# Expert products in source order: gate and up by turns, and expert 0's gather one row block ahead

## The chip, the cores and the metric

The kernel runs on one core of one Trainium2 chip. The metric is device time in microseconds (us), taken over runs of the same program.

## The reference, cut to what matters

One layer over 512 latent tokens of width 1024 with 256 context tokens: a mixer (projection, recurrence, attention, output projection), then routed experts. The change touches only the experts. Each of 16 experts takes the 64 tokens that score highest for it, and its three weight matrices (1024 x 2816, 1024 x 2816, 2816 x 1024, float32) are read once.

```
def expert_choice_ffn(h, w_router, w_gate, w_up, w_down):
    aff = jax.nn.softmax((h @ w_router).astype(jnp.float32), axis=-1)
    g, idx = lax.top_k(jnp.swapaxes(aff, 1, 2), cap)          # cap = 64
    xe = jax.vmap(lambda hb, ib: hb[ib])(h, idx)
    def expert(args):
        xk, wg, wu, wd = args
        return (jax.nn.silu(xk @ wg) * (xk @ wu)) @ wd
    ...
```

## The kernel before, in words

Up to about 448 us the mixer and the router run; their instructions are recorded in a `Flow` object and issued in the order of its list schedule (helper line 254 in the profile). Then come the experts.

The weights of an expert come in 24 loads, issued by SP (SyncE): for each of eight row blocks k (128 rows of the gate and of the up matrix) one load of gate and one of up, then eight loads of the down matrix, three blocks of 128 rows in each but the last. Each load fills one of 14 slots of SBUF, taken in turn (`slot`); a load waits until the products that read its slot's former content are done. One expert is 34.6 MB (3 x 1024 x 2816 x 4 bytes).

`gather` builds the input of two experts at once: for each of the eight k, four products with a one-hot matrix (`oh`), made by eight VectorE instructions, into a PSUM bank (`y` and `tr` by turns), and a ScalarE instruction that writes `xe[:, k]`. `gates` takes the gate values and the token numbers by small products and VectorE copies.

`up_part` multiplies: for each k, for each of six chunks of columns (five of 512, one of 256), for hh = 0 (gate) and 1 (up), one product into the bank `gu` of that chunk. Gate writes PSUM partitions 0 to 63 of the bank, up writes 64 to 127, so the two use different halves of TensorE's columns:

```
pe.matmul(b[hh * 64:(hh + 1) * 64, :n], xe[:, k, es], wgu[k][hh][:, f:f + n],
          start=(k == 0), stop=(k == KT - 1), skip_group_check=True)
```

A float32 product stands in the trace as two passes, so a row block's 12 products are 24 passes.

`down_part` takes each chunk through SiLU (ScalarE), the multiply by up (VectorE), transposes (TensorE, bank `tr`) and a copy to `hT` (ScalarE); then 22 times two products with the down weights go into the bank `y`, each pair to the two halves; then the scaling (VectorE) and an indirect DMA from GpSimd that adds the 64 rows to the output.

What sets the order: expert 0's gather and `up_part` are recorded in the `Flow`, with a `bias` that falls by 100 for each k, and go out in its list schedule. From expert 0's `down_part` on, instructions are given straight to the engines outside of a manual schedule, and the framework's scheduler may put those of one engine in another order than they are written.

Of the kernel before, what the change touches and what calls it, by code (L numbers as in the profile page):

```python
# [42 lines left out]
class Flow:  # L43
    """Records the instructions of a phase, orders them by a list schedule of their data
    dependences and issues them in that order; Tile still draws every wait."""
# [78 lines left out]
    def copy(self, o, i):  # L124
        """A copy on whichever of ScalarE and VectorE is free first."""
        self.add("act", "activation", (o, i, AF.Copy), {}, [("vec", "tensor_copy", (o, i), {})])

    def affine(self, o, i, scale, bias):
        """scale * i + bias, a column each, on ScalarE or VectorE."""
        self.add("act", "activation", (o, i, AF.Identity), {"scale": scale, "bias": bias},  # L130
                 [("vec", "tensor_scalar", (o, i, scale, bias), {"op0": OP.mult, "op1": OP.add})])

    def tt(self, o, a, b, op):
        """A tensor_tensor in SBUF on whichever of VectorE and GpSimd is free first."""
        self.add("vec", "tensor_tensor", (o, a, b), {"op": op}, [("gp", "tensor_tensor", (o, a, b), {"op": op})])
# [88 lines left out]
    def flush(self):  # L224
        """Issues what was recorded in the order of a list schedule, by the longest path to the end."""
        ops, self.ops = self.ops, []
        for name, op in self.waits:
            for rec in self.acc[name]:
                self.link(rec[0], op)
        self.waits = []  # L230
        deps = {o["i"]: o["n"] for o in ops}
        topo = [o for o in ops if not o["n"]]
        for o in topo:
            for s, _ in o["to"].values():
                deps[s["i"]] -= 1
                if not deps[s["i"]]:
                    topo.append(s)
        assert len(topo) == len(ops)
        for op in reversed(topo):
            c = min(v[3] for v in op["alt"].values())  # L240
            if op["e"] == "sp":
                c += 2.5 + op["bytes"] / 360e3
            op["c"] = c
            op["lvl"] = op["boost"] + max([c, 0.0] + [s["lvl"] + (0.0 if issue else c)
                                                      for s, issue in op["to"].values()])
        for op in ops:
            op["lvl"] += op["bias"]
        order, self.free, self.dma_free, self.act_set = self.schedule(ops)
        for o, e, st, end in order:
            o["e"], o["st"], o["end"] = e, st, end  # L250
            o["m"], o["a"], o["k"], o["cost"] = o["alt"][e]
        with self.tc.manual_schedule():
            for o, e, st, end in order:
                getattr(self.eng[e], o["m"])(*o["a"], **o["k"])  # L254
# [58 lines left out]
def hybrid_block_kernel(ctx: ExitStack, tc: tile.TileContext, x, cx, w_ada, b_ada, w_in, w_out, w_router, w_gate,  # L313
# [23 lines left out]
    def carve(slot):  # L337
        """Small tiles out of a slot that the experts' weights take over."""
        flat, end = slot.rearrange("p a d -> p (a d)"), [0]

        def part(shape):
            n = int(np.prod(shape[1:]))
            v = flat[:shape[0], end[0]:end[0] + n]
            end[0] += n
            assert end[0] <= 3 * D
            dims = "abc"[:len(shape) - 1]
            return v if len(shape) == 2 else v.rearrange(f"p ({' '.join(dims)}) -> p {' '.join(dims)}",
                                                         **{d: k for d, k in zip(dims, shape[1:])})
        return part
# [18 lines left out]
    def load_ex(e, k, i):  # L368
        """Rows of an expert's gate (i = 0) or up weights."""
# [24 lines left out]
    def split(h, l, src):  # L394
        """src as the sum of two float32r parts."""
        copy(h, src)
        tt(l, src, h.bitcast(F32), OP.subtract)

# [61 lines left out]
    # start clears the accumulation flags of its whole bank, so only the first product in a bank sets it  # L460
    def chan_chunk(w, with_ctx, kouter=False):
        """Two channel tiles of 512 latent tokens, a bank each, and their 256 context tokens in a third one."""
# [119 lines left out]
    def tok_chunk(w, with_ctx):  # L582
        """256 columns of two token tiles to a bank."""
# [34 lines left out]
    # tables of the rotary embedding with the norms' gains, [token, tile, dim]  # L618
# [31 lines left out]
    # softplus(-lambda) as max(-lambda, 0) + 2 atanh(t / (2 + t)), t = exp(-|lambda|)  # L650
# [92 lines left out]
    def qk_post(v, t, tb, kind, dst):  # L743
        """Norm and rotation of token tiles t, t + 1 in bank v, 256 columns each; keys as float32r parts, transposed."""
# [194 lines left out]
    # w_out as two float32r parts in place of the input projection's operands  # L939
# [19 lines left out]
    def mix_parts(t, parts):  # L959
        """The mixer's output for token tile t as float32r parts; parts: (tiles of lru and att, H, L)."""  # L960
# [63 lines left out]
    # logits = rstd * (x1 (A2 w)) + B2 w  # L1024
# [37 lines left out]
    # the 64 largest, sorted, of the first two tiles, then of these and the third tile, and of the fourth tile  # L1062
# [31 lines left out]
    # of two sorted rows the 64th largest is the largest of min(i-th of one, (64 - i)-th of the other)  # L1094
# [18 lines left out]
    # tokens above the least one taken, and of those equal to it the first ones, as many as are left to take  # L1113
# [15 lines left out]
    def count(o, m, stop):  # L1129
        """How many tokens up to each one have m, for each expert."""  # L1130
# [13 lines left out]
    # over the norms, by which the gathering products are scaled  # L1144
# [21 lines left out]
    def gather(pair):  # L1166
        """The tokens of two experts, normed and modulated, one column each."""
        xe = E.tile([128, KT, 128], F32, name="xe", bufs=1)
# [5 lines left out]
        for k in range(KT):  # L1174
            flow.bias = 2050.0 - 100 * k
            pg = etr([128, 128]) if k % 2 else pe_ps.tile([128, 128], F32, name="y", tag="y", bufs=1)
            for t in range(4):
                pe.matmul(pg, X1[t][:, k * 128:(k + 1) * 128], oh[:, t].rearrange("p i s -> p (i s)"),  # L1178
                          start=(t == 0), stop=(t == 3))
            act.activation(xe[:, k], pg, AF.Identity, bias=B2[:, k:k + 1], scale=A2[:, k:k + 1])  # L1180
        flow.bias = 0.0
        return xe, oh

    def gates(pair, oh):
        """The gate values of the taken tokens of two experts (twice, below each other) and the tokens' numbers."""
# [16 lines left out]
    def up_part(xe, i, wgu):  # L1202
        gu = [pe_ps.tile([128, 512], F32, name="gu", tag="gu", bufs=6) for _ in FC]
        es = slice(i * CAP, (i + 1) * CAP)
        for k in range(KT):
            flow.bias = 2000.0 - 100 * k
            for (f, n), b in zip(FC, gu):
                for hh in range(2):
                    pe.matmul(b[hh * 64:(hh + 1) * 64, :n], xe[:, k, es], wgu[k][hh][:, f:f + n],  # L1209
                              start=(k == 0), stop=(k == KT - 1), skip_group_check=True)  # L1210
        flow.bias = 0.0
        return gu

    def down_part(gu, wd, g_t, ix):
        hT = E.tile([128, NF, CAP], F32, name="hT", tag="hT", bufs=1)
        y = pe_ps.tile([128, 512], F32, name="y", tag="y", bufs=1)
        for (f, n), b in zip(FC, gu):
# [7 lines left out]
        for ff in range(NF):  # L1225
            for hh in range(2):
                pe.matmul(y[hh * 64:(hh + 1) * 64, :], hT[:, ff], wd[ff][:, hh * 512:(hh + 1) * 512],  # L1227
                          start=(ff == 0), stop=(ff == NF - 1), skip_group_check=True)
# [7 lines left out]

    wgu, wd = load_gu(0), load_dn(0)
    xe, oh = gather(0)
    gu = up_part(xe, 0, wgu)
    gx = gates(0, oh)  # L1240
    flow.flush()
    act, vec, gp, pe, sp = nc.scalar, nc.vector, nc.gpsimd, nc.tensor, nc.sync
    down_part(gu, wd, *gx[0])
    for e in range(1, NE):
        wgu, wd = load_gu(e), load_dn(e)
        cur = gx[e % 2]
        gu = up_part(xe, e % 2, wgu)
        if e % 2 == 1 and e + 1 < NE:
            xe, oh = gather((e + 1) // 2)
            gx = gates((e + 1) // 2, oh)  # L1250
        down_part(gu, wd, *cur)
# [9 lines left out]
def _layout(inputs):  # L1261
    """The small parameters side by side, as the kernel loads them."""
# [4 lines left out]
    # [channel tile, block of the tile, in, direction, gate, out]  # L1267
# [37 lines left out]
```

## Time and profile before

| | |
|---|---|
| median of 3 runs | 1779.17 us (1779.17, 1779.17, 1780.07) |
| profiled execution, first to last instruction | 1780.5 us |
| PE (TensorE products) busy | 1644.3 us, 92% |
| DVE (VectorE), ACT (ScalarE), POOL (GpSimd) busy | 387.6, 323.0, 132.5 us |
| bytes moved by DMA | 607.33 MB |
| granted TensorE clock, mean | 0.969 |

The profiled execution's span is its own time; it is 0.07% above the median of the runs shown, and sums are made against it. A busy PE is not a PE at its peak, since the ends of products are modelled. SP's busy time is not counted; its queue is seen in the timeline of its issues. A granted clock of 1.00 is 2.4 GHz, 0.50 is 1.2 GHz.

### The profile page before, as it was taken

Reading aid. Unit: us, or ns where it says so; the run is one execution under the profiler, and the core shown is the slowest. Engines: PE = TensorE matmul, PEld = TensorE weight load, DVE = VectorE, ACT = ScalarE, POOL = GpSimd, SP = SyncE. Lnnn points to the kernel's source line nnn. Section 1 sums busy time; section 2 is a strip of 40 time slices with the busy share of each in tenths; the row PEclk is TensorE's granted clock in tenths of the full one; section 3 lists DMA queues with packets and bytes.
Section 4 is the critical chain, followed back from the end, with each engine's and each line's share of the span. In section 5 each row is a group of like instructions: output and inputs, shape, how many; then the busy total and the mean of one; then the engine's idle time right before and its main releaser. Section 6 shows DMA issues by size and latency. Waiting matters only on the chain.

```text
span 1780.5 us, 19112 instructions
## 1 busy us (share of the span) xinstructions
PE 1644.3 (92%) x8030; PEld 798.7 (45%) x8030; DVE 387.6 (22%) x788; ACT 323.0 (18%) x607; POOL 132.5 (7%) x143
## 2 busy tenths in 40 slices
PE   7999988883899999999999999999999999999997
PEld 4567787672433433344343334333433433343332
DVE  5667786724110100010010001010100010000001
ACT  5256755520010101020010102010100101020101
POOL 2141153300000000000000000000000000000000
PEclk9999999896899999999999999999999999999999
DMA  9563112255689999999999999999999999999997
GB/s 346 173 225 107 36 36 83 78 190 207 260 324 363 419 401 423 417 426 416 420 420 423 421 422 420 422 414 426 420 420 420 423 420 420 423 420 422 421 422 293
DMA packets 116900, 607.33 MB, mean 341 GB/s; under 512 B 12393, under 2 KB 31046, under 8 KB 84046
## 3 DMA queue, kind: packets, MB, share of 16 engines
q1 hardware_dynamic: 115534, 601.91, 83.1%
q0 software_dynamic: 1280, 4.20, 1.2%
q8 instruction: 63, 1.03, 0.2%
q14 instruction: 23, 0.19, 0.0%
HBM read 599.78 MB, written 6.29 MB: 340 GB/s over the span
## 4 chain that ended last, share of the span: by engine, by line
PE 49%; DMA 35%; issue 6%; DVE 6%; ACT 2%; POOL 1%; SPq 0%; POOLq 0%; ACTq 0%; DVEq 0%
PE gu L1209 18%; DMA r<-in_w_up_dram 16%; DMA ring<-in_w_up_dram 9%; PE y L1227 9%; PE ac L254 7%; DMA r<-in_w_down_dram 5%; PE gu L254 3%; DMA ring<-in_w_down_dram 3%; PE pv L254 3%; PE p L254 2%; PE tr L254 1%; PE tr L1223 1%; PE y L1178 1%; DVE ring L254 1%; PE tr L1178 1%
## 5 line engine op out<-in xcount | busy, mean ns | idle before, releaser
L1209 PE MATMUL gu<-r,xe 128*64 128x512 f32 (+1 forms) x1656 | 479.6, 560 | 5.9 <-DMA r<-in_w_up_dram 4.9
L1209 PE MATMUL gu<-ring,xe 128*64 128x512 f32 (+1 forms) x1224 | 365.8, 560 | 3.2 <-DMA ring<-in_w_up_dram 3.2
L1209 PEld LDWEIGHTS gu<-r,xe 128*64 128x64 f32 x1656 | 173.9, 137 | 275.9 <-issue 252.9
L1220 DVE TENSOR_TENSOR sg<-sg,gu 64x512 f32<-64x512 f32 x96 | 61.7, 647 | 785.3 <-ACT sg L1219 785.1
L1219 ACT ACTIVATE sg<-gu 64x512 f32<-64x512 f32 x96 | 52.7, 553 | 984.6 <-PE gu L1209 977.7
L1209 PEld LDWEIGHTS gu<-ring,xe 128*64 128x64 f32 x1224 | 131.4, 136 | 202.1 <-issue 187.1
L1227 PE MATMUL y<-r,hT 128*64 128x512 f32 x812 | 210.3, 617 | 0.6 <-DMA r<-in_w_down_dram 0.6
L1227 PE MATMUL y<-ring,hT 128*64 128x512 f32 x596 | 151.7, 606 | 1.2 <-DMA ring<-in_w_down_dram 1.2
L1234 POOL DMA_INDIRECT out_dram<-ys,ix x16 | 22.8, 1426 | 1313.2 <-DVE ys L1233 1313.2
L254 PE MATMUL ac<-w,ring 128*128 128x256 f32 x768 | 108.2, 290 | 1.1 <-DVE w L254 0.7
L1227 PEld LDWEIGHTS y<-r,hT 128*64 128x64 f32 x812 | 58.8, 139 | 99.3 <-issue 90.3
L254 PEld LDWEIGHTS ac<-w,ring 128*128 128x128 f32 x768 | 97.4, 190 | 12.8 <-issue 11.2
L1233 DVE SCALAR_TENSOR_TENSOR ys<-y,gate,brow 64x512 f32<-64x512 f32 x32 | 24.0, 749 | 294.9 <-PE y L1227 294.6
L1227 PEld LDWEIGHTS y<-ring,hT 128*64 128x64 f32 x596 | 43.7, 138 | 75.5 <-issue 69.0
L254 PE MATMUL ac<-ring,w 128*128 128x512 f32 (+1 forms) x240 | 68.4, 395 | 0.2 <-ACT V L254 0.2
L1223 PEld LDWEIGHTS tr<-ident,sg 64*128 64x128 f32 x352 | 30.5, 145 | 77.7 <-ACT hT L1224 40.6
L1223 PE MATMUL tr<-ident,sg 64*128 64x64 f32 x352 | 43.7, 244 | 13.8 <-ACT hT L1224 8.3
L1224 ACT ACTIVATE hT<-tr 128x256 f32<-128x256 f32 x96 | 35.1, 366 | 103.5 <-PE tr L1223 97.8
L254 PEld LDWEIGHTS ac<-ring,w 128*128 128x128 f32 x240 | 40.9, 194 | 8.6 <-issue 3.4
L1178 PE MATMUL y<-oh,raw 128*128 128x128 f32 x224 | 31.0, 281 | 14.6 <-DVE ys L1233 10.4
L254 ACT ACT_TABLE_LOAD x32 | 41.1, 1283 | 8.1 <-DVE lru L254 6.8
L254 PE MATMUL p<-kS,qs 128*128 128x256 f32 (+1 forms) x128 | 33.7, 378 | 5.4 <-ACT e L254 5.4
(250 smaller groups left out, 1263.7 us busy)
## 6 DMA issues: line engine op xcount, KB each, us to landing
r<-in_w_gate_dram SPq DMA_DIRECT2D x73, 1408.0 KB, 26.0
r<-in_w_up_dram SPq DMA_DIRECT2D x73, 1408.0 KB, 26.6
r<-in_w_down_dram SPq DMA_DIRECT2D x64, 1536.0 KB, 21.1
ring<-in_w_gate_dram SPq DMA_DIRECT2D x55, 1408.0 KB, 25.9
ring<-in_w_up_dram SPq DMA_DIRECT2D x55, 1408.0 KB, 26.5
ring<-in_w_down_dram SPq DMA_DIRECT2D x47, 1536.0 KB, 20.9
raw<-in_w_ada_dram SPq DMA_DIRECT2D x32, 512.0 KB, 4.7
raw<-in_w_in_dram SPq DMA_DIRECT2D x20, 512.0 KB, 4.7
```

The costliest lines, as they stand in the source:

```text
L254: getattr(self.eng[e], o["m"])(*o["a"], **o["k"])
L1178: pe.matmul(pg, X1[t][:, k * 128:(k + 1) * 128], oh[:, t].rearrange("p i s -> p (i s)"), start=(t == 0), stop=(t == 3))
L1209: pe.matmul(b[hh * 64:(hh + 1) * 64, :n], xe[:, k, es], wgu[k][hh][:, f:f + n], start=(k == 0), stop=(k == KT - 1), skip_group_check=True)
L1219: act.activation(sg[64:128, :n], b[:64, :n], AF.Silu)
L1220: vec.tensor_tensor(sg[64:128, :n], sg[64:128, :n], b[64:128, :n], op=OP.mult)
L1223: pe.transpose(pt[:, j], sg[64:128, j * 128:(j + 1) * 128], ident[64:128, 64:128])
L1224: act.activation(hT[:, f // 128:f // 128 + n // 128], pt[:, :n // 128], AF.Copy)
L1227: pe.matmul(y[hh * 64:(hh + 1) * 64, :], hT[:, ff], wd[ff][:, hh * 512:(hh + 1) * 512], start=(ff == 0), stop=(ff == NF - 1), skip_group_c ...
L1233: vec.scalar_tensor_tensor(ys[:, cs_], y[pp, :], g_t[pp, :], m5row[pp, :], op0=OP.mult, op1=OP.mult)
L1234: gp.indirect_dma_start(out=out, out_offset=bass.IndirectOffsetOnAxis(ap=ix[:, :1], axis=0), in_=ys, in_offset=None, compute_op=OP.add)
```

## The change

Three things. Expert 0's gather and products are no longer recorded in the `Flow`: they are written out as gather block 0, then for each k gather block k + 1 and the products of row block k. All expert work is put inside a manual schedule, so that each engine gets its instructions as written: gate and up by turns in every chunk, the gather for the next two experts as one piece after an odd expert's row blocks. And `down_part` writes the down products of chunk c - 1 behind chunk c's transposes and copy. The mixer, the router, the loads' order on SP and the arithmetic are the same.

```
-    def up_part(xe, i, wgu):
-        gu = [pe_ps.tile([128, 512], F32, name="gu", tag="gu", bufs=6) for _ in FC]
+    def up_rows(gu, xe, i, wgu, k):
         es = slice(i * CAP, (i + 1) * CAP)
-        for k in range(KT):
-            flow.bias = 2000.0 - 100 * k
-            for (f, n), b in zip(FC, gu):
-                for hh in range(2):
-                    pe.matmul(b[hh * 64:(hh + 1) * 64, :n], xe[:, k, es], wgu[k][hh][:, f:f + n],
-                              start=(k == 0), stop=(k == KT - 1), skip_group_check=True)
+        for (f, n), b in zip(FC, gu):
+            for hh in range(2):
+                pe.matmul(b[hh * 64:(hh + 1) * 64, :n], xe[:, k, es], wgu[k][hh][:, f:f + n],
+                          start=(k == 0), stop=(k == KT - 1), skip_group_check=True)
...
             act.activation(hT[:, f // 128:f // 128 + n // 128], pt[:, :n // 128], AF.Copy)
-        for ff in range(NF):
-            for hh in range(2):
-                pe.matmul(y[hh * 64:(hh + 1) * 64, :], hT[:, ff], wd[ff][:, hh * 512:(hh + 1) * 512],
-                          start=(ff == 0), stop=(ff == NF - 1), skip_group_check=True)
+            if c:
+                products(*FC[c - 1])
+        products(*FC[-1])
...
     wgu, wd = load_gu(0), load_dn(0)
-    xe, oh = gather(0)
-    gu = up_part(xe, 0, wgu)
-    gx = gates(0, oh)
+    oh = one_hot(0)
     flow.flush()
     act, vec, gp, pe, sp = nc.scalar, nc.vector, nc.gpsimd, nc.tensor, nc.sync
-    down_part(gu, wd, *gx[0])
-    for e in range(1, NE):
-        wgu, wd = load_gu(e), load_dn(e)
-        cur = gx[e % 2]
-        gu = up_part(xe, e % 2, wgu)
-        if e % 2 == 1 and e + 1 < NE:
-            xe, oh = gather((e + 1) // 2)
-            gx = gates((e + 1) // 2, oh)
-        down_part(gu, wd, *cur)
+    with tc.manual_schedule():
+        for e in range(NE):
+            if e == 0:
+                xe, gu = new_xe(), banks()
+                gather(xe, oh, 0)
+                for k in range(KT):
+                    if k + 1 < KT:
+                        gather(xe, oh, k + 1)
+                    up_rows(gu, xe, 0, wgu, k)
+                gx = gates(0, oh)
+                cur = gx[0]
+            else:
+                wgu, wd = load_gu(e), load_dn(e)
+                cur = gx[e % 2]
+                gu = banks()
+                for k in range(KT):
+                    up_rows(gu, xe, e % 2, wgu, k)
+                if e % 2 == 1 and e + 1 < NE:
+                    oh = one_hot((e + 1) // 2)
+                    xe = new_xe()
+                    for k in range(KT):
+                        gather(xe, oh, k)
+                    gx = gates((e + 1) // 2, oh)
+            down_part(gu, wd, *cur)
```

What this does to the order on PE, at expert 0's row block 3 (`ring1_3763` is its gate block, `ring1_3764` its up block, `gu_...` the six banks). Before:

```order
L254 MATMUL gu_3791<-ring1_3763,xe_3781 64x512
L254 MATMUL gu_3792<-ring1_3763,xe_3781 64x512
L254 MATMUL gu_3793<-ring1_3763,xe_3781 64x512
L254 MATMUL gu_3794<-ring1_3763,xe_3781 64x512
L254 MATMUL gu_3795<-ring1_3763,xe_3781 64x512
L254 MATMUL gu_3796<-ring1_3763,xe_3781 64x256
L254 MATMUL gu_3791<-ring1_3764,xe_3781 64x512
L254 MATMUL gu_3792<-ring1_3764,xe_3781 64x512
L254 MATMUL gu_3793<-ring1_3764,xe_3781 64x512
L254 MATMUL gu_3794<-ring1_3764,xe_3781 64x512
L254 MATMUL gu_3795<-ring1_3764,xe_3781 64x512
L254 MATMUL gu_3796<-ring1_3764,xe_3781 64x256
```

The same row block with the change:

```order
L1209 MATMUL gu_3843<-ring1_3763,xe_3842 64x512
L1209 MATMUL gu_3843<-ring1_3764,xe_3842 64x512
L1209 MATMUL gu_3844<-ring1_3763,xe_3842 64x512
L1209 MATMUL gu_3844<-ring1_3764,xe_3842 64x512
L1209 MATMUL gu_3845<-ring1_3763,xe_3842 64x512
L1209 MATMUL gu_3845<-ring1_3764,xe_3842 64x512
L1209 MATMUL gu_3846<-ring1_3763,xe_3842 64x512
L1209 MATMUL gu_3846<-ring1_3764,xe_3842 64x512
L1209 MATMUL gu_3847<-ring1_3763,xe_3842 64x512
L1209 MATMUL gu_3847<-ring1_3764,xe_3842 64x512
L1209 MATMUL gu_3848<-ring1_3763,xe_3842 64x256
L1209 MATMUL gu_3848<-ring1_3764,xe_3842 64x256
```

Six gate products and then six up products became pairs of the two. Before, 3 of the 128 row blocks stood fully by turns (one in expert 0, its block 5), 56 fully one after the other, the rest in between; now all 128 stand by turns.

The second place is ScalarE at the end of expert 0's row blocks (`sg` is the SiLU's result, `hT` the transposed chunk, `tr` the bank of the transposes). Before:

```order
L1219 ACTIVATE sg_4019<-gu_3791 64x512
L1219 ACTIVATE sg_4028<-gu_3792 64x512
L1224 ACTIVATE hT_4017<-tr_4022 128x256
L1219 ACTIVATE sg_4037<-gu_3793 64x512
L1224 ACTIVATE hT_4017<-tr_4031 128x256
```

With the change:

```order
L1224 ACTIVATE sg_4021<-gu_3843 64x512
L1229 ACTIVATE hT_4019<-tr_4024 128x256
L1224 ACTIVATE sg_4030<-gu_3844 64x512
L1229 ACTIVATE hT_4019<-tr_4033 128x256
L1224 ACTIVATE sg_4047<-gu_3845 64x512
```

The second chunk's SiLU stood ahead of the first chunk's copy to `hT`, and now stands behind it. So it is in every expert.

## Rows read from the trace of the kernel before

**Rows 1.** The page, section 2: mean busy share of the DMA engines in 40 slices:
```profile
DMA  9563112255689999999999999999999999999997
```

**Rows 2.** Stretches: length, busy us of PE, PEld, DVE, ACT, POOL, clock, DMA share, GB/s:
```profile
460.00:540.00 80.00, 76.30 (x314) 30.94 (x312) 6.10 (x18) 9.99 (x20) 0.00 (x0) 0.96 0.77 294
480.00:500.00 20.00, 20.00 (x69) 7.97 (x67) 0.00 (x0) 0.91 (x2) 0.00 (x0) 1.00 0.99 376
540.00:640.00 100.00, 97.22 (x469) 40.49 (x466) 7.78 (x20) 9.06 (x20) 1.77 (x1) 0.97 1.00 409
640.00:1740.00 1100.00, 1058.70 (x4663) 420.29 (x4662) 83.54 (x170) 92.51 (x204) 19.65 (x14) 0.99 1.01 421
```

**Rows 3.** Timeline of SP's queue, 440 to 545: start, us, the loads it issues:
```profile
464.29 0.33 SPq L254 DMA_DIRECT2D ring<-in_w_gate_dram  x1
...
472.87 9.49 SPq L254 DMA_DIRECT2D r<-in_w_down_dram  x4
...
506.72 0.34 SPq L371 DMA_DIRECT2D r<-in_w_gate_dram  x1
...
525.49 0.33 SPq L371 DMA_DIRECT2D ring<-in_w_up_dram  x1
537.49 0.33 SPq L371 DMA_DIRECT2D r<-in_w_gate_dram  x1
```

**Rows 4.** Chain of waits, 440 to 545 us: start, us, engine, tile, line, count:
```profile
457.14 7.53 PE gu L254 x23
...
482.93 8.36 PE gu L254 x23
...
501.83 4.87 PE gu L254 x24
...
507.79 6.64 PE gu L254 x23
...
525.16 0.30 PE gu L254
```

**Rows 5.** Short stretches in expert 0, same columns as rows 2:
```profile
460.00:465.00 5.00, 5.00 (x21) 1.94 (x18) 0.00 (x0) 0.00 (x0) 0.00 (x0) 1.00 0.00 0
465.00:470.00 5.00, 5.00 (x21) 2.16 (x21) 0.00 (x0) 0.46 (x1) 0.00 (x0) 1.00 0.93 349
530.00:535.00 5.00, 5.00 (x14) 1.55 (x15) 1.38 (x2) 1.56 (x5) 0.00 (x0) 0.50 0.13 52
```

**Rows 6.** Page, section 6: loads by tile, count, KB each, us to landing:
```profile
r<-in_w_gate_dram SPq DMA_DIRECT2D x73, 1408.0 KB, 26.0
```

**Rows 7.** Chain of waits, 440 to 545 us, first down products of expert 0:
```profile
530.19 3.60 PE y L1227 x6
```

**Rows 8.** Page, section 5: SiLU and gating multiply, busy, mean ns, idle before:
```profile
L1220 DVE TENSOR_TENSOR sg<-sg,gu 64x512 f32<-64x512 f32 x96 | 61.7, 647 | 785.3 <-ACT sg L1219 785.1
L1219 ACT ACTIVATE sg<-gu 64x512 f32<-64x512 f32 x96 | 52.7, 553 | 984.6 <-PE gu L1209 977.7
```

**Rows 9.** Timeline of PE, last expert: start, us, line, tiles, count, idle before:
```profile
1743.67 4.94 PE L1209 MATMUL gu<-r,xe 128*64 128x512 f32 x18 [0.22 <-DMA r<-in_w_up_dram]
...
1749.52 0.46 PE L1223 MATMUL tr<-ident,sg 64*128 64x64 f32 x4 [0.52 <-ACT hT L1224]
...
1766.20 5.37 PE L1227 MATMUL y<-r,hT 128*64 128x512 f32 x24 [0.29 <-DMA r<-in_w_down_dram]
1771.40 1.03 PE L1227 MATMUL y<-ring,hT 128*64 128x512 f32 x4
```

**Rows 10.** Chain of waits, 1600 to 1700 us:
```profile
1634.06 26.94 DMA ring<-in_w_up_dram
```

**Rows 11.** A stretch of the last expert's rows, same columns as rows 2:
```profile
1700.00:1720.00 20.00, 18.95 (x70) 6.58 (x67) 0.00 (x0) 0.00 (x0) 0.00 (x0) 1.00 1.01 429
```

**Rows 12.** Chain of waits, 600 to 640 us: gather for experts 2 and 3:
```profile
605.31 1.16 PE y L1178 x8
...
614.54 0.69 PE tr L1223 x4
```

More of the change, by code (lines that the diff above doesn't have):

```diff
@@ L1164, in load_dn, with one_hot @@
         return res
-    def gather(pair):
-        xe = E.tile([128, KT, 128], F32, name="xe", bufs=1)
+    def one_hot(pair):
         oh = E.tile([128, 4, 2, CAP], F32, name="oh", bufs=1)
@@ L1173, in gather @@
                 vec.tensor_scalar(oh[:, t, i], slots, sl, rs2[:, t:t + 1], op0=OP.is_equal, op1=OP.mult)
-        for k in range(KT):
[L1175 to L1182, printed above, removed]
+        return oh
+    def gather(xe, oh, k):
+        pg = etr([128, 128]) if k % 2 else pe_ps.tile([128, 128], F32, name="y", tag="y", bufs=1)
+        for t in range(4):
+            pe.matmul(pg, X1[t][:, k * 128:(k + 1) * 128], oh[:, t].rearrange("p i s -> p (i s)"),
+                      start=(t == 0), stop=(t == 3))
+        act.activation(xe[:, k], pg, AF.Identity, bias=B2[:, k:k + 1], scale=A2[:, k:k + 1])
     def gates(pair, oh):
@@ L1200, in hybrid_block_kernel, with banks @@
     FC = [(f, min(512, FE - f)) for f in range(0, FE, 512)]
-    def up_part(xe, i, wgu):
-        gu = [pe_ps.tile([128, 512], F32, name="gu", tag="gu", bufs=6) for _ in FC]
+    def banks():
+        return [pe_ps.tile([128, 512], F32, name="gu", tag="gu", bufs=6) for _ in FC]
+    def up_rows(gu, xe, i, wgu, k):
         es = slice(i * CAP, (i + 1) * CAP)
-        for k in range(KT):
-            flow.bias = 2000.0 - 100 * k
-            for (f, n), b in zip(FC, gu):
-                for hh in range(2):
-                    pe.matmul(b[hh * 64:(hh + 1) * 64, :n], xe[:, k, es], wgu[k][hh][:, f:f + n],
-                              start=(k == 0), stop=(k == KT - 1), skip_group_check=True)
-        flow.bias = 0.0
-        return gu
+        for (f, n), b in zip(FC, gu):
+            for hh in range(2):
+                pe.matmul(b[hh * 64:(hh + 1) * 64, :n], xe[:, k, es], wgu[k][hh][:, f:f + n],
+                          start=(k == 0), stop=(k == KT - 1), skip_group_check=True)
     def down_part(gu, wd, g_t, ix):
@@ L1216, in down_part, with products @@
         y = pe_ps.tile([128, 512], F32, name="y", tag="y", bufs=1)
-        for (f, n), b in zip(FC, gu):
+        def products(f, n):
+            for ff in range(f // 128, (f + n) // 128):
+                for hh in range(2):
+                    pe.matmul(y[hh * 64:(hh + 1) * 64, :], hT[:, ff], wd[ff][:, hh * 512:(hh + 1) * 512],
+                              start=(ff == 0), stop=(ff == NF - 1), skip_group_check=True)
+        for c, ((f, n), b) in enumerate(zip(FC, gu)):
             sg = E.tile([128, 512], F32, name="sg", bufs=2)
@@ L1235, in down_part, with new_xe @@
                               in_offset=None, compute_op=OP.add)
+    def new_xe():
+        return E.tile([128, KT, 128], F32, name="xe", bufs=1)
     wgu, wd = load_gu(0), load_dn(0)
-    xe, oh = gather(0)
-    gu = up_part(xe, 0, wgu)
-    gx = gates(0, oh)
+    oh = one_hot(0)
     flow.flush()
     act, vec, gp, pe, sp = nc.scalar, nc.vector, nc.gpsimd, nc.tensor, nc.sync
-    down_part(gu, wd, *gx[0])
-    for e in range(1, NE):
-        wgu, wd = load_gu(e), load_dn(e)
-        cur = gx[e % 2]
-        gu = up_part(xe, e % 2, wgu)
-        if e % 2 == 1 and e + 1 < NE:
-            xe, oh = gather((e + 1) // 2)
-            gx = gates((e + 1) // 2, oh)
-        down_part(gu, wd, *cur)
+    with tc.manual_schedule():
[22 more added lines that the diff above has]
+            down_part(gu, wd, *cur)
     for p_ in (pe_ps, E, R3, R2, R0, R1, P0, X):
```

## The prediction

> **What bounds the kernel now.** I read the 40 slices of the page first: from slice 13 to the last but one the DMA share is 9, and the dips lie before, in the mixer and around 400 to 540 us [rows 1]. Then I cut the experts into stretches. From 640 to 1740 us the DMA engines are busy at a share of 1.01 and move 421 GB/s; from 540 to 640 it is 1.00 and 409; from 460 to 540 only 0.77 and 294 [rows 2]. An expert has 34.6 MB, which at 421 GB/s is 82.2 us, and 15 experts of that are most of the run. The chain of waits late in the run agrees: it goes through loads of up weights, 26.94 us in one piece, not through products [rows 10]. So for 1100 us the stream of weights is the bound, and a product made faster there only waits longer. What the stream lost is in the 80 us before 540, where a share of 0.77 is 0.23 x 80 = 18.4 us of idle DMA engines.
>
> Who held them up there is seen in SP's queue beside the chain. Nothing moves from 460 to 465 [rows 5], because the last row block of expert 0 (k = 7) takes the slots of its first, and SP issues it at 464.29, when the first block's gate products are done [rows 3]. The down weights follow at 472.87, as the next blocks end, and expert 1's first at 506.72. A second hole, share 0.13 from 530 to 535 [rows 5], lies between an issue at 525.49 and one at 537.49 [rows 3]: the latter waits for the first down products of expert 0, and these come only after its row blocks end at 525.5 (525.16 + 0.30) [rows 4]. The chain through that time is PE's own: 7.53 us for the first block, 8.36 for block 3, 4.87 for block 5, 6.64 for block 6 [rows 4]. Block 5 is the one that stood fully by turns before; block 3 had six gate products and then six up products. This is the price of the order: 8.36 against 4.87 us for the same 24 passes at a granted clock of 1.00 [rows 2].
>
> **Expert 0's row blocks.** All eight now stand by turns, 4.87 us each. A gather block comes with it: block 5 starts at 501.83 and block 6 at 507.79, so row block and gather together take 5.96 us [rows 4]. From the same start, 457.14: first block 4.87, six with a gather 35.8, the last 4.87, end at 502.6 instead of 525.5, 22.8 us earlier. The first block's slots come free at 457.14 + 4.87 = 462.0 instead of 464.3.
>
> The two column halves are worth a factor 8.36 / 4.87 = 1.72 here [rows 4]. The Trainium skill, TensorEngine Tiling (Array Packing), section Theoretical Speedup, says up to 2 where a dimension is 64 or less. By that a block would be 4.18 us, the first slots would come free 0.7 us sooner, and the gain below would be larger by that 0.7; the measured 4.87 is used.
>
> **The stream.** I make the sum in bytes. From 460 to 640 the kernel before moves 0.294 x 80 + 0.409 x 100 = 64.4 MB [rows 2]. Before, it restarted 1.1 us behind SP's issue at 464.29 [rows 3]: nothing from 460 to 465, and a share of 0.93 from 465 to 470, so from 465.35 [rows 5]. With the issue at 462 it restarts at about 463.0. From then on PE frees two slots every 5.96 us, that is 2.88 MB (two loads of 1408 KB [rows 6]), a demand of 484 GB/s, more than the 421 of the steady stream. The queue fills and the stream does not run dry until expert 0's last row block.
>
> How fast does it run there? It is not shown with a filling queue. The lower bound is the rate of 480 to 500 us, when the engines were busy (0.99) and moved 376 GB/s; the upper bound is 421 [rows 2]. I take 376 for the first 32 us, to 495, while few loads are queued, as they were in that row, and 421 after: 12.0 MB + 52.4 MB / 0.421 = 32 + 124.4 us, end at 619.4 instead of 640. **Gain 20.6 us.** With 421 throughout the 64.4 MB take 153.0 us from 463.0, a gain of 24.0. If only idle time goes and the rates stay, 18.4 us of idle shrink to the 3.0 us from 460 to 463, a gain of 15.4. These are the ends.
>
> **The end of expert 0.** All gate-value products now come behind the last row block, and its first down products before were 12.0 us behind that (525.5 to the issue at 537.49 [rows 3, 4]). The same distance from 502.6 is 514.6. By then the queue holds the k = 7 pair, the down weights and three pairs of expert 1, 2.9 + 11.5 + 8.7 = 23.1 MB from 463.0; they last 55 us at 421 GB/s, to 517.9, or 61 at 376. So the second hole closes, if narrowly.
>
> **Waits that the change adds.** ScalarE's second SiLU now stands behind the first chunk's copy, which waits for PE's transposes. Queued behind it are that chunk's multiply on VectorE and its transposes, for which PE waits. Before, PE stood 0.52 us between the first two chunks [rows 9]; now about 0.4 for the copy, 0.55 and 0.65 for SiLU and multiply [rows 8], and handing over, 2.0 in all, **1.5 us more per expert**. Later chunks have 16 passes of down products over the same chain (at 5.37 / 24 = 0.22 us a pass, 3.6 us [rows 9]). In odd experts the multiply also stands behind the copies of the gate values, another 1 us or so. An up product that stands between gate products makes PE wait for the up load before it goes on with gate; before, the gate half could run ahead. After the last load this costs nothing: 4.94 us remained then [rows 9], and 4.87 do now. Fifteen of the sixteen times all this lies under the stream. Two experts now need of PE 16 x 4.87 + 9.2 for a gather (605.31 to 614.54 [rows 12]) + 2 x 23.8 from the last row block to the last down pass (1748.6 to 1772.4 [rows 9]) + 4 = 139 us, and the stream 164. In the last expert it is on the path, but PE there also waited 0.29 us for down weights [rows 9], and its interleaving had small gaps of its own. I take **+1.0 us**, with 0 and 3 as ends; 3 is a slow start on top, as before, where six passes took 3.60 us instead of 1.3 [rows 7].
>
> VectorE's one-hot work, the gather's ScalarE writes and GpSimd's scatter keep their number. They are under the stream, with PE's 25 us of room per pair of experts as the cover. SP's list of loads is the same, and no queue gets another DMA to pass.
>
> **Sum.** 1780.5 - 20.6 + 1.0 = 1760.9 us against the profiled execution, which is 0.07% over the median of 1779.17; against that median **1759.6 us**. The ends: 1779.2 - 24.0 + 0 = 1755, and 1779.2 - 15.4 + 3 = 1767.
>
> **Rivals.** *The hole at expert 0's end stays.* If the in-order start of the down part costs some 5 us more than before, SP's issue comes after the queue has drained, and idle time as from 530 on, up to 7.9 us, is back: 1760 + 8 = 1768 us. For it: the margin above is 3 us at the fast rate. Against: the slower the rate, the larger the margin.
>
> *The stream never gets faster than it was.* If the whole stretch runs at what its busy time gave (23.5 MB in 61.6 us, 381 GB/s), 64.4 MB take 169 us from 463.0, to 632, a gain of 8: 1772 us. Against it stand 409 and 421 right behind [rows 2].
>
> *The clock falls (slower).* PE needs 4.87 us of every 6.85 that a pair of loads takes, so it now stands idle in each row block. At 530 PE came from a pause, the clock was 0.50 [rows 5], and six passes took 2.3 us more [rows 7]. If each row block paid that, it would take 7.2 us; PE sets the pace from 6.5 on (4.87 + (164 - 139) / 16), and the loss is 0.7 x 16 x 7.5 pairs = 84 us, less the gain: 1843 us. Against: in the last expert PE waited for loads block after block, and the clock stayed 1.00 [rows 11]; the pauses were shorter, though, since the old order took more of the time. A PE that falls behind also stops pausing. [...]
>
> *The halves don't overlap (slower).* If blocks by turns took 8.36 us after all, expert 0 would end near 530 and lose some 5 us: 1784. Block 5 speaks against it [rows 4].
>
> **How the numbers follow.** A measurement of this kernel can tell about 0.2%, 3.6 us, from no change. Forecast 0.74, with its own range 1755 to 1767; the hole stays 0.10; the slower stream 0.06; something that eats all but 3.6 us of the gain 0.04; clock 0.04; halves 0.02. The range from 1753 to 1769 takes the forecast's ends, a little for the steady stream's own rate on the fast side, and the first rival. Faster 0.74 + 0.10 + 0.06 = 0.90, same 0.04, slower 0.06.
>
> **What would show it.** Right: row blocks of expert 0 at 4.9 us, its last near 503; SP's issue of the k = 7 pair near 462; share 0.95 or more from 465 to 540; still 421 GB/s from 640 on, with PE busy falling and its waits for up loads rising. Wrong: a hole left between 510 and 530, a granted clock well under 1.00 in late row blocks, or a rate under 415 GB/s there.

## The result and the profile after

The changed kernel takes **1756.69 us** (median of 4 runs, 1755.81 to 1757.96), the kernel before on the same chip 1779.17 us (1775.41 to 1780.07). The ratio is 0.988, with a 95% interval of 0.9866 to 0.9895, that is 18.7 to 23.8 us less. The forecast was 1759.6 us with a range of 1753 to 1769.

The profiled execution of the changed kernel spans 1754.3 us, 26.2 less than that of before. Part of this is not the change's: mixer and router, whose code is the same, end at slightly other times from one execution to the next. So below times in the experts count from the router's last reduction on VectorE (`least`), which starts at 448.33 us in the execution of before and at 443.35 in that of after. From there to the end before takes 1332.2 us and after 1310.9: **21.2 us of the 26.2 lie in the experts**; the medians of the runs differ by 22.5.

Section 2 of the page, the line of [rows 1]. Before has 5, 6 and 8 in slices 10 to 12 of 40; here the same slices read 5, 6 and 9, and from slice 12 (482 us) to the last but one no dip is left:

```profile
DMA  9573102255699999999999999999999999999997
```

The stretches of [rows 2], of after (length, busy us of PE, PEld, DVE, ACT, POOL, then granted clock, DMA share, GB/s):

```profile
460.00:540.00 80.00, 76.66 (x412) 30.35 (x410) 7.69 (x20) 9.08 (x18) 1.76 (x1) 0.96 1.01 415
480.00:500.00 20.00, 19.59 (x132) 8.71 (x128) 0.22 (x2) 2.79 (x4) 0.00 (x0) 1.00 1.03 423
540.00:640.00 100.00, 96.07 (x526) 40.81 (x523) 6.50 (x13) 9.75 (x21) 1.43 (x1) 0.97 1.01 420
640.00:1740.00 1100.00, 911.60 (x4590) 350.07 (x4587) 87.00 (x181) 98.22 (x214) 18.23 (x13) 0.96 1.01 420
```

Most of the gain stands in the first row: 415 GB/s where before moved 294, or 319 from 465 to 545 us, which is as far behind `least`. Behind 640 us the stream runs as before, 420 GB/s against 421, and PE's busy time there falls from 1058.7 to 911.6 us without buying anything. Where most of those 147 us went is seen in section 5 of the page (busy, mean ns, idle just before and what ended it). Before:

```profile
L1209 PE MATMUL gu<-r,xe 128*64 128x512 f32 (+1 forms) x1656 | 479.6, 560 | 5.9 <-DMA r<-in_w_up_dram 4.9
L1209 PE MATMUL gu<-ring,xe 128*64 128x512 f32 (+1 forms) x1224 | 365.8, 560 | 3.2 <-DMA ring<-in_w_up_dram 3.2
```

After:

```profile
L1209 PE MATMUL gu<-r,xe 128*64 128x512 f32 (+1 forms) x1752 | 396.7, 573 | 87.3 <-DMA r<-in_w_up_dram 83.3
L1209 PE MATMUL gu<-ring,xe 128*64 128x512 f32 (+1 forms) x1320 | 301.6, 569 | 58.8 <-DMA ring<-in_w_up_dram 56.4
```

PE now waits 83.3 + 56.4 = 139.7 us for loads of up weights, before 4.9 + 3.2. The faster row blocks of experts 1 to 15 are waited away.

Expert 0's row blocks in the chain of waits, as in [rows 4] (start, us, engine, tile, line, count; `y` and `tr` at L1179 are gather blocks):

```profile
448.74 2.14 PE y L1179 x8
450.88 1.71 PE tr L1179 x8
452.58 5.51 PE gu L1209 x24
458.10 1.09 PE y L1179 x8
459.18 4.87 PE gu L1209 x24
464.06 1.09 PE tr L1179 x8
465.15 4.87 PE gu L1209 x24
...
489.00 9.60 PE gu L1209 x48
...
504.13 5.75 PE y L1219 x16
...
510.27 3.58 PE y L1219 x16
```

The first block takes 5.51 us, the next five 4.87 each with 1.09 of gather between them, the last two 9.60 together. The last ends at 489.00 + 9.60 = 498.6, which is 55.2 us after `least`; before it was 525.5, 77.1 after.

SP's queue, as in [rows 3]:

```profile
458.12 0.33 SPq L254 DMA_DIRECT2D ring<-in_w_gate_dram  x1
...
464.08 6.87 SPq L254 DMA_DIRECT2D r<-in_w_down_dram  x4
...
487.93 0.34 SPq L371 DMA_DIRECT2D r<-in_w_gate_dram  x1
...
509.06 0.33 SPq L371 DMA_DIRECT2D r<-in_w_gate_dram  x1
```

The first row is the gate load of the k = 7 pair, 14.8 us behind `least` (before 16.0); four down loads then go out in 6.87 us instead of 9.49, and expert 1's first pair 44.6 us behind `least` instead of 58.4. The last row waits for the first down products of expert 0. What it waits for no longer costs anything, as two short stretches show:

```profile
500.00:510.00 10.00, 7.07 (x30) 2.58 (x28) 2.29 (x5) 1.94 (x4) 0.00 (x0) 0.66 1.01 430
510.00:520.00 10.00, 10.00 (x54) 3.60 (x55) 1.81 (x3) 2.70 (x6) 0.00 (x0) 1.00 1.01 427
```

The hole of [rows 5] at 530 to 535 has no counterpart: the share is 1.01 right through.

The last expert on PE, as in [rows 9]:

```profile
1710.06 4.50 PE L1209 MATMUL gu<-ring,xe 128*64 128x512 f32 x20 [1.73 <-DMA ring<-in_w_up_dram]
...
1716.87 4.94 PE L1209 MATMUL gu<-r,xe 128*64 128x512 f32 x22 [1.87 <-DMA r<-in_w_up_dram]
1721.74 0.46 PE L1228 MATMUL tr<-ident,sg 64*128 64x64 f32 x4
1724.05 0.46 PE L1228 MATMUL tr<-ident,sg 64*128 64x64 f32 x4 [1.85 <-DVE sg L1225]
...
1744.99 1.03 PE L1219 MATMUL y<-ring,hT 128*64 128x512 f32 x4
```

PE waits 1.73 and 1.87 us for an up load in the last row blocks, and 1.85 us between the first two chunks' transposes (0.52 before). From the start of the last row block to the end of the last down pass it takes 1746.02 - 1716.87 = 29.15 us, before 1772.43 - 1743.67 = 28.76.

### The profile page after: what moved, and what is told of

Its sections match the earlier page's. It is cut to its first block, busy times and chain, and to the rows that moved or that the text cites. A ratio compares the mean times of both kernels' runs of the same rounds, so it can differ in the third digit from the quotient of the medians.

```text
span 1754.3 us, 19030 instructions
## 1 busy us (share of the span) xinstructions
PE 1477.0 (84%) x8030; PEld 723.1 (41%) x8030; DVE 386.9 (22%) x788; ACT 324.4 (18%) x607; POOL 131.8 (8%) x143
## 3 DMA queue, kind: packets, MB, share of 16 engines
q8 instruction: 63, 1.03, 0.2%
## 4 chain that ended last, share of the span: by engine, by line
DMA 48%; PE 36%; issue 6%; DVE 6%; ACT 2%; POOL 1%; SPq 0%; POOLq 0%; ACTq 0%; DVEq 0%
DMA r<-in_w_up_dram 21%; DMA ring<-in_w_up_dram 16%; PE gu L1209 11%; PE ac L254 7%; PE y L1219 7%; DMA r<-in_w_down_dram 5%; DMA ring<-in_w_down_dram 4%; PE pv L254 3%; PE p L254 3%; PE y L1179 2%; PE tr L1179 1%; PE tr L254 1%; PE po L254 1%; DVE ring L254 1%; PE tr L1228 1%
## 5 line engine op out<-in xcount | busy, mean ns | idle before, releaser
L1209 PE MATMUL gu<-r,xe 128*64 128x512 f32 (+1 forms) x1752 | 396.7, 573 | 87.3 <-DMA r<-in_w_up_dram 83.3
L1209 PE MATMUL gu<-ring,xe 128*64 128x512 f32 (+1 forms) x1320 | 301.6, 569 | 58.8 <-DMA ring<-in_w_up_dram 56.4
L1209 PEld LDWEIGHTS gu<-r,xe 128*64 128x64 f32 x1752 | 134.2, 140 | 332.0 <-issue 206.5
L1219 PE MATMUL y<-r,hT 128*64 128x512 f32 x812 | 200.6, 635 | 2.2 <-DMA r<-in_w_down_dram 2.1
L1209 PEld LDWEIGHTS gu<-ring,xe 128*64 128x64 f32 x1320 | 103.1, 139 | 239.0 <-issue 149.1
L1219 PE MATMUL y<-ring,hT 128*64 128x512 f32 x596 | 145.7, 628 | 1.7 <-DMA ring<-in_w_down_dram 1.7
L1181 ACT ACTIVATE xe<-y,B,A 128x128 f32<-128x128 f32 x32 | 14.6, 457 | 473.1 <-PE y L1179 473.1
```

## The experiments

Two theories stood behind the runs. **Theory A**: the gain is expert 0's alone. Its row blocks by turns free their slots faster, so that the stream of weights does not run dry; everything else in the change is covered by the stream or costs a little in the last expert. **Theory B**: a good part comes from elsewhere, from the order of the 15 other experts, the gather as one piece, or down products between chunks.

This table sets the profiled executions on one footing. The issue is SP's of the k = 7 gate load. The kernel before, run beside them, took 1779.17 us for the change, 1777.58 for the next four rows and 1778.32 for the last two:

| kernel | `least` starts | issue behind it | `least` to the end of the span | median of runs, us |
|---|---|---|---|---|
| before | 448.33 | 15.96 | 1332.2 | 1779.17 |
| the change | 443.35 | 14.77 | 1310.9 | 1756.69 |
| expert 0 alone | 443.17 | 14.63 | 1310.5 | 1756.89 |
| expert 0 not by turns | 444.51 | 14.60 | 1334.9 | 1781.38 |
| other experts not by turns | 446.00 | 14.24 | 1395.4 | 1842.33 |
| two chunks ahead | 445.74 | 14.79 | 1311.0 | 1758.63 |
| gather blocks first | 445.78 | 20.11 | 1315.3 | 1763.69 |
| row block 0 first | 447.44 | 15.73 | 1313.9 | 1761.82 |

### Expert 0's part alone

The kernel before, with expert 0's gather and row blocks as in the change; the rest is left to the scheduler as before:

```
-    xe, oh = gather(0)
-    gu = up_part(xe, 0, wgu)
-    gx = gates(0, oh)
...
+    with tc.manual_schedule():
+        xe = E.tile([128, KT, 128], F32, name="xe", bufs=1)
+        gu = [pe_ps.tile([128, 512], F32, name="gu", tag="gu", bufs=6) for _ in FC]
+        gather_k(xe, oh, 0)
+        for k in range(KT):
+            if k + 1 < KT:
+                gather_k(xe, oh, k + 1)
+            up_rows(gu, xe, 0, wgu, k)
+        gx = gates(0, oh)
```

> The kernel before, with expert 0's gather and row blocks alone written as in the change (gate and up by turns, gather one block ahead); experts 1 to 15 and all down parts are left to the scheduler as before. Theory A (the stream of weights is the bound after 540 us, and the whole gain is that expert 0 frees its slots earlier): all of the gain is there, 1754 to 1760 us, and the DMA share from 460 to 540 is 0.95 or more. Theory B (every expert's faster products count): a sixteenth of the gain, 1777 to 1779 us. Theory C (gain shared between expert 0 and the in-order down parts): about 1768 us.

Measured: 1756.89 us (1755.49 to 1758.04) against 1777.58 of before, ratio 0.9882 (0.9865 to 0.99). The stretches of its profile:

```profile
460.00:540.00 80.00, 78.72 (x420) 32.41 (x417) 7.78 (x20) 9.08 (x18) 1.77 (x1) 0.98 1.01 415
640.00:1700.00 1060.00, 1018.15 (x4484) 401.98 (x4481) 82.15 (x168) 92.66 (x204) 18.23 (x13) 0.99 1.02 421
```

The same 415 GB/s in the first stretch, and PE as busy as before in the second: all of the gain with none of the 147 us of saved PE time. From `least` to the end it is 1310.5 us, the change's within 0.4. Theories B and C fall.

### Expert 0 not by turns, the rest as in the change

```
+        for hh in range(2):
+            for (f, n), b in zip(FC, gu):
+                pe.matmul(b[hh * 64:(hh + 1) * 64, :n], xe[:, k, es], wgu[k][hh][:, f:f + n],
...
-                    up_rows(gu, xe, 0, wgu, k)
+                    up_rows_apart(gu, xe, 0, wgu, k)
```

> The changed kernel, but in expert 0 each row block has its six gate products first and then its six up products; experts 1 to 15 stand by turns. Theory A: expert 0's row blocks take 8.4 us each and end some 5 us later than in the kernel before, so the gain is lost and a little more: 1780 to 1788 us, with holes in the stream between 460 and 545 us. Theory B: fifteen sixteenths of the gain stay, 1757 to 1759 us.

Measured: 1781.38 us (1776.91 to 1784.14, 12 runs), ratio 1.0019 (1.0009 to 1.0029). The gain is gone. The chain and a stretch show how:

```profile
463.66 8.36 PE gu L1216 x23
472.02 1.09 PE tr L1179 x8
473.11 8.36 PE gu L1216 x23
```

```profile
460.00:540.00 80.00, 76.66 (x293) 30.83 (x293) 3.20 (x8) 7.54 (x14) 0.00 (x0) 0.96 0.81 296
480.00:500.00 20.00, 20.00 (x69) 8.00 (x67) 0.00 (x0) 0.92 (x2) 0.00 (x0) 1.00 0.89 331
```

The second fence tells something about rates. A row block and a gather block take 9.45 us here and free two slots for down loads of 1536 KB, 3.15 MB: a demand of 333 GB/s, and from 480 to 500 us the DMA engines move 331. Over all eight down loads, 11.5 MB (the last has 512 KB), SP's issues stretch from 468.56 us to expert 1's first at 506.34: 305 GB/s asked, 306 moved. In the kernel before they stretch from 472.87 to 506.72: 341 asked, 342 moved. In both the stream takes what PE frees. In the change the same pair of slots comes free every 5.96 us, a demand of 528 GB/s (the prediction had 484, with the size of gate loads), and the stream gives 423 from 480 to 500 us.

### The other experts not by turns

The same edit in experts 1 to 15, with expert 0 by turns.

> The changed kernel, but experts 1 to 15 have the six gate products of a row block first and then the six up products. Theory A: PE has room for row blocks of up to about 6.5 us; at 7 us (as such blocks seem to follow each other in the trace of before) PE sets the pace at 173 us per pair of experts instead of 164, 1820 us; at 8.4 us 195 us per pair, 1985 us; DMA share falls to 0.85 to 0.95. Rival (the stream hides any order of these products): 1757 us.

Measured: 1842.33 us (1840.67 to 1844.01), ratio 1.0359 (1.0339 to 1.0378). The order by turns brings nothing for these experts, but not every other order is hidden: the scheduler's mixture was, in the run with expert 0 alone; six and then six in every block is not. The chain of waits in the middle of the run no longer passes a load:

```profile
973.51 57.07 PE gu L1216 x177
...
1054.35 57.07 PE gu L1216 x177
1111.42 1.09 PE y L1179 x8
...
1125.10 4.96 PE y L1226 x16
...
1147.54 57.07 PE gu L1216 x177
```

Eight row blocks take 57.07 us, 7.13 each. One expert without a gather takes 1054.35 - 973.51 = 80.84 us, the next with one 1147.54 - 1054.35 = 93.19, together 174.0, where the stream needs 164.4 for two. PE sets the pace, and the sum over the run agrees: expert 1's rows start at 529.33 in the chain, seven experts with a gather and eight without give 1299.1 us, so the last down pass should end near 1828; it ends at 1833.1. The expected 1820 us was too low: the pairs took 174.0 us and not 173, and the change, to which the loss is added, needs only 1218.7 us from expert 1's first product (527.37 us) to the last down pass, 14 less than 7.5 pairs of 164.4. The DMA share from 640 to 1700 us is 0.97, above the expected 0.85 to 0.95. By turns, PE is busy for 879.0 of the 1060 us from 640 to 1700, 136 us of a pair's 164.

### Two chunks' SiLU and multiply ahead

The change, with the second chunk's SiLU and multiply written before the first chunk's copy, and so on one ahead; it takes the 1.85 us pause away.

```
+        sgs = [gated(0), gated(1)]
...
+            if c + 2 < len(FC):
+                sgs.append(gated(c + 2))
```

> The changed kernel, with the SiLU and multiply of two chunks issued ahead of the first chunk's copy to hT, and of chunk c + 2 behind the copy of chunk c. Theory A: PE's pause between the first two chunks falls from 1.85 us to about 0.5 in every expert, and the time only by what stands in the last expert, 1 to 1.5 us: about 1755.4 us. Rival (PE's pauses add up over the experts): sixteen times 1.35 us, 1735 us.

Measured: 1758.63 us (1756.73 to 1763.2), ratio 0.9897 (0.988 to 0.9914): no gain. Its last expert on PE:

```profile
1719.26 4.94 PE L1209 MATMUL gu<-r,xe 128*64 128x512 f32 x22 [1.85 <-DMA r<-in_w_up_dram]
...
1725.11 0.46 PE L1233 MATMUL tr<-ident,sg 64*128 64x64 f32 x4 [0.52 <-ACT hT L1234]
...
1738.01 2.80 PE L1219 MATMUL y<-r,hT 128*64 128x512 f32 x12 [0.52 <-DMA r<-in_w_down_dram]
1741.78 1.08 PE L1219 MATMUL y<-r,hT 128*64 128x512 f32 x4 [0.97 <-DMA r<-in_w_down_dram]
...
1747.40 1.03 PE L1219 MATMUL y<-ring,hT 128*64 128x512 f32 x4
```

The pause is 0.52 again, and 0.52 + 0.97 us of waiting for down weights stand in its place, where the change has 0.23. From the last row block's start to the end of the last pass it is 1748.43 - 1719.26 = 29.17 us against 29.15: even in the last expert PE waits for the stream, so most of the pause that the change adds there is covered. The expectation of 1755.4 was wrong by leaving the down loads out.

### Where expert 0's gather stands

Both kernels move the gather blocks of expert 0 alone. In the first all eight stand ahead of the row blocks:

```
-                gather(xe, oh, 0)
                 for k in range(KT):
-                    if k + 1 < KT:
-                        gather(xe, oh, k + 1)
+                    gather(xe, oh, k)
+                for k in range(KT):
                     up_rows(gu, xe, 0, wgu, k)
```

> The change, but all eight gather blocks of expert 0 stand before its first row block, which then follow each other by turns without gather work between them. Theory A (what the change gains is the time at which expert 0's row blocks free their slots, and the rate behind that is PE's pace or the stream's 421 GB/s, whichever is less): in the changed kernel two gather blocks and a first row block of 5.51 us lie before the release of the k = 6 and k = 7 slots; with all eight gather blocks first (six more of 1.1 to 1.7 us) SP's issue of the k = 7 pair comes 6 to 9 us later against the least reduce of the mixer than in the changed kernel. The DMA engines stand idle that much longer, and the blocks behind follow at 4.87 us, so the stream then runs at its own rate; 1763 us, 6 to 8 slower than the change. Rival (the place of the gather is free, since the row blocks come faster once they start, and only their form by turns counts): 1757 us, within 2 of the change.

Measured: 1763.69 us (1763.18 to 1767.37), ratio 0.9924 (0.9905 to 0.9944). Its products on PE, from the third gather block on:

```profile
454.81 1.72 PE L1179 MATMUL y<-oh,raw 128*128 128x128 f32 x8
456.37 1.06 PE L1179 MATMUL tr<-oh,raw 128*128 128x128 f32 x8
...
460.93 4.94 PE L1209 MATMUL gu<-ring,xe 128*64 128x512 f32 x24
465.70 9.62 PE L1209 MATMUL gu<-r,xe 128*64 128x512 f32 x48
```

The issue comes 5.3 us later behind `least` (20.11 against 14.77) and the end 4.4 later (1315.3 against 1310.9); the medians differ by 7.0, with 2.4 of later mixer in the profiled execution. The six gather blocks cost less than expected, since the last five follow each other by 0.89 us. The time and the order of events are Theory A's: the end follows the moment at which the first slots come free, although the last row block even ends 2 us sooner behind `least` than in the change.

In the second, built on the kernel with two chunks ahead, row block 0 stands ahead of gather block 1:

```
+                up_rows(gu, xe, 0, wgu, 0)
+                gather(xe, oh, 1)
+                for k in range(1, KT):
```

> The change with two chunks' SiLU and multiply ahead of the first copy, and with expert 0's row block 0 ahead of its gather block 1 (gather 0, rows 0, gather 1, gather 2, rows 1 and so on). Theory A (each us by which the first row block ends sooner restarts the stream sooner, and the steady stream behind it passes that on): a gather block of about 1.7 us no longer stands before the first row block's end, but PE may wait for ScalarE's write of the gathered block, which it did not before; SP's issue of the k = 7 pair 0.7 to 1.7 us earlier against the least reduce, and 1 to 2 us less than the kernel with the two chunks ahead alone: 1755.5 to 1757.5. Rival (the wait for ScalarE's write takes the place of the gather block on PE, so nothing comes sooner): no difference, 1757 to 1758.6.

Measured: 1761.82 us (1759.18 to 1763.14), ratio 0.9902 (0.9883 to 0.9921). A miss: neither expectation has this time. The issue came 0.9 us later than in the kernel with two chunks ahead, not earlier, and the timeline of PE and two stretches of the first row block say why:

```profile
455.57 7.57 PE L1209 MATMUL gu<-ring,xe 128*64 128x512 f32 x24 [0.61 <-ACT xe L1181]
```

```profile
455.57:459.30 3.73, 3.73 (x10) 1.25 (x12) 0.00 (x0) 0.00 (x0) 0.00 (x0) 0.50 0.14 60
459.30:463.10 3.80, 3.80 (x17) 1.04 (x13) 0.00 (x0) 0.00 (x0) 0.00 (x0) 0.79 0.00 0
```

The same in the change, its two gather blocks and then the first row block:

```profile
448.74:452.51 3.77, 3.77 (x16) 3.55 (x16) 1.28 (x6) 0.46 (x1) 0.00 (x0) 0.50 0.86 365
452.51:455.30 2.79, 2.79 (x11) 0.95 (x12) 0.00 (x0) 0.46 (x1) 0.00 (x0) 0.76 0.00 0
455.30:458.10 2.80, 2.80 (x17) 0.92 (x13) 0.00 (x0) 0.00 (x0) 0.00 (x0) 1.00 0.00 0
```

PE comes from the router's waits at a granted clock of 0.50. In the change the two gather blocks run at 0.50, and the row block behind them, at 0.76 and then 1.00, takes 5.51 us. Here the row block itself runs at 0.50 and 0.79 and takes 7.57, and PE waits 0.61 us for ScalarE's write of the gathered block besides. Two gather blocks then stand ahead of row block 1, so the second slots come free 1.8 us later (SP's down loads 22.6 us behind `least` against 20.8). In the profiled executions the end comes 2.9 us later, 1.1 more than that, which stays open. Whether the kernel is slower than the one with two chunks ahead is not told by the runs, whose intervals overlap; nothing shows it faster.

None of these kernels beats the change; expert 0's part alone equals it.

## Why the prediction was right, point by point

**The bound and the place of the gain: right.** The stream of weights sets the end, the only idle time to win lay between 460 and 540 us, and expert 0's row blocks by turns win it. The run with expert 0 alone shows that its part suffices, the run with expert 0 not by turns that the order by turns is needed in it.

**Row blocks of 4.87 us and a period of 5.96: right** for all but the first (the last two took 4.80 each). The first took 5.51, and its first half ran at a mean granted clock of 0.76; and it started 9.2 us behind `least` instead of 8.8, since gather block 1 now stands whole before it. So the first slots came free 1.2 us sooner, not the 2.3 of "462.0 instead of 464.3". In the time of before, the issue is at 463.1 and the restart, 1.1 behind it, at 464.2.

**The mis-sized term: "I take 376 for the first 32 us".** The stream ran at 395 GB/s in the first 32 us from the restart (459.2 to 491.2 us), and at 412 from the restart to 540 as a whole. What was read as a rate of the DMA engines with few loads queued stood in a stretch that went at PE's pace of freeing slots, 341 GB/s asked and 342 moved over all the down loads. The busy share of 0.99 in that row of [rows 2] misled: with the faster row blocks the same 20 us have 1.03 and 423 GB/s. Expert 0 not by turns shows the same coupling at 305 asked and 306 moved. The rival of 381 GB/s throughout falls with it.

The sum with measured terms: of the 64.4 MB, 33.3 move in 80.8 us at 412 GB/s from 464.2 and the other 31.1 in 74.0 us at 420, end at 619.0 instead of 640, a gain of 21.0; the last expert takes 0.4 more; **20.6 us net, and 21.2 were measured**. The rates are rounded to 1 GB/s, which over such a stretch is 0.4 us and over the 1100 us behind it, at 421 and 420, more than 2, so the sum is not better than that. The prediction had 20.6 - 1.0 = 19.6. The later end of the first block cost 1.2 of it, the faster stream gave 1.6 back, the last expert 0.6: that these partly cancel is luck; the mechanism was right.

**The second hole closes: right.** The share is 1.01 from 500 to 520 us. The rival that had it stay is out.

**Added waits, "+1.0 us": right in kind, too large.** 1.85 us between the first two chunks, 2.0 predicted; but at the end only 0.4 us more. The run with two chunks ahead takes the pause away and gets waits for down loads in its place.

**PE's room: right.** 139 us of work in a pair's 164 was worked out and 136 busy measured; the threshold of 6.5 us a row block lies between 4.87, which costs nothing, and 7.13, which costs 85 us.

**The clock rival: refuted.** PE waits up to 1.87 us in the last row blocks, and the clock stays where [rows 11] had it:

```profile
1700.00:1720.00 20.00, 14.67 (x74) 5.25 (x72) 0.69 (x1) 0.59 (x1) 0.00 (x0) 1.00 1.01 421
```

PE busy fell from 18.95 to 14.67 us of these 20, and the granted clock is still 1.00. The Trainium skill, TensorE: Matmul & The Clock Gate, section Loop structure matters more than you think, warns of a long wait for a DMA ahead of each product, behind which PE goes cold. At waits of 1.73 and 1.87 us the trace shows no such fall. From 640 to 1740 us the mean granted clock did fall a little, from 0.99 to 0.96. Where it falls is seen behind expert 0's row blocks: PE is busy for 1.07 of 4 us with small products, and then the clock is 0.50:

```profile
500.00:504.00 4.00, 1.07 (x11) 0.82 (x8) 1.60 (x4) 0.97 (x2) 0.00 (x0) 0.70 1.00 425
504.00:508.00 4.00, 4.00 (x12) 1.24 (x12) 0.69 (x1) 0.97 (x2) 0.00 (x0) 0.50 1.02 434
```

There the first 16 down passes take 5.75 us instead of 3.58, under the stream and at no cost. **Halves that don't overlap** are refuted by 4.87 against 8.36 us in the same place (expert 0 not by turns).

## What to carry to other kernels

When a stream of loads sets the end, look for the stretch where it runs dry and for the engine that frees its buffers there: here a faster order in that stretch was worth all, and the same order elsewhere nothing, as long as the engine's work per load stayed below the load's own time. Before a rate of the DMA engines is used as a limit, divide the bytes of the slots by the time in which the engine ahead frees them; where the two agree, the row shows demand and not capacity. And behind the router's pause PE ran at the low clock at first, so a small piece was better there than the one that releases the loads.

## What was not expected of the hardware

Six gate products and then six up products of a row block take 8.36 us with a gather block behind it, but 7.13 us a block where such blocks follow each other. By turns it is 4.87 with a gather block behind it and about 4.8 where blocks follow each other (9.60 us for two). That the end of one group overlaps with the start of the next on the other column half would explain it; no run here shows that by itself.

The DMA engines' busy share is 0.99 at 376 GB/s in [rows 2] and 1.03 at 423 in the same stretch of the change. The share alone does not tell how much more could be moved.
